# Two heads of a pair on opposite halves of the rows in a chunked RWKV-7 recurrence

## The chip, the cores and the metric

The kernel runs on one core of a Trainium2 chip, in one launch. The metric is the device time of that launch in microseconds (us). PE is the matrix engine with its 128 x 128 array, DVE, ACT and POOL are the vector, scalar and GpSimd engines, and SP issues most of the transfers.

## What is computed

One layer of a hybrid block on x of shape 1 x 2048 x 1024 in float32: an input projection, an S5 branch, an RWKV-7 branch, a gated merge of both, an output projection and a feed-forward layer of width 4096. The change concerns the recurrence of the RWKV-7 branch alone, which has 8 heads of width 64 and goes over 2048 frames:

```python
def step(state, inp):
    rt, wt, kt, vt, at, bt = inp
    sa = jnp.einsum('bhvk,bhk->bhv', state, at)
    state = (state * wt[:, :, None, :] + sa[..., None] * bt[:, :, None, :]
             + vt[..., None] * kt[:, :, None, :])
    yt = jnp.einsum('bhvk,bhk->bhv', state, rt)
    return state, yt
```

Before it stand element-wise steps that make r, the decay, k, v, a and b; behind it a normalization over each head, a bonus term and a gate.

## The kernel before

The program runs in four phases one after the other: `phase_a` (input projection and S5), `phase_b` (the recurrence, and beside it the two gate projections), `phase_c` (merge and output projection) and `phase_d` (feed-forward). Large products are made as three products of split float32 numbers (`mm3`, lines 121 to 123).

`phase_b` goes over 16 steps s of 128 frames, that is two chunks c = 0, 1 of 64 frames. Three generators work on a step, each one step later than the one ahead of it: `elem(s)` makes the operands AR (a and r, scaled by the decay), BK (b and k) and the rest; `inv(s)` makes what depends on one chunk alone; `chain(s)` carries the state. A fourth, `gates()`, makes the products `gp` of the gate projections, 512 columns each and 24 to a bank, from lines 121 to 123. `robin` (line 82) takes one stretch up to the next `yield` from each generator in turn, in the order chain, gates, elem, inv; so the small products of the recurrence stand between gate products on PE. Within a stretch a scheduler may move instructions, except those wrapped in `pin`, which stay in program order and show line 677, the line of the wrapper.

The 8 heads are 4 pairs h with e = 0, 1: head e of a pair has its 64 channels on rows 64e to 64e+63 of AR, BK and the state SB. What `inv(s)` makes for both chunks:

- `m` (line 782): the products of BK with AR of one chunk, 4 pairs by 2 heads, into one bank for each e. The stationary operand is 64 rows (one head's channels) by 128 columns (b and k frames), 128 columns stream. DVE masks them into TM[c] (line 785). The order of b and k in BK turns with c, so chunk 0 has its k frames on rows 0 to 63 and its b frames on rows 64 to 127, chunk 1 the other way round.
- `vt` (line 804): v transposed to frames by channels, all 128 frames and both heads of a pair at once, four products with a 128 x 128 stationary operand and 128 columns. ACT copies 64 rows for each chunk into VU (line 807).
- `NC`, `YC`, `Y`, `X`: the inverse of the chunk's triangular matrix, its 16 x 16 diagonal blocks on DVE (lines 813, 815) by way of transfers through `inv_d`, the rest in `levels(s)` by 64 x 64 and 32 x 32 products P and D.
- `kb` (line 831): the transpose of BK of one chunk to frames by channels, four full 128 x 128 transposes, copied to KB.
- `mv` (line 838): what the chunk's own k and v add, in MV.

`halves(c)` gives the half of the rows that holds the k and v frames of chunk c, and the opposite half, here called its update half, that holds its b frames and the updates u. In the kernel before all 8 heads of a chunk use the same update half. `chain(s)` does for each of the two chunks in turn, n = 2s + c:

- `R` (line 901): four products, one a pair, 128 rows by 64 columns stationary, 128 columns streaming, so that the zeros off the diagonal blocks of SB keep the heads apart. DVE adds MV (line 903) on the 64 rows of the update half, 512 columns.
- `U` (line 907): 8 products of 64 x 64 with Y, all in the one block of the array that has the update half as rows and as columns. ACT copies the 64 rows, 512 columns, into the update half of VU (line 909).
- `S` (line 916), `y` (lines 923, 924): the new state's sum and the outputs, 128 rows by 64 columns stationary, the two heads of a pair in opposite column halves. DVE writes the new state (line 928), POOL has scaled the old one ahead of that (line 898).

The PSUM banks that `m`, `vt`, `kb`, `mv` and some others use come from one pool of two, those of R, U and S from a pool of one.

Of the kernel before, what the change touches and what calls it, by code (L numbers as in the profile page):

```python
# [610 lines left out]
def phase_b(tc, nc, K, io, pm_d, ob_d, h_d, gt_d, gs_d, inv_d):  # L611
    V, A, P, T = nc.vector, nc.scalar, nc.gpsimd, nc.tensor
    NS = S // 128
    with ExitStack() as st:
# [145 lines left out]

        def halves(c):

            return slice(64 * c, 64 * c + 64), slice(64 - 64 * c, 128 - 64 * c)

        def quarters(c):
# [2 lines left out]
        def inv(s):  # L768
# [6 lines left out]
            for c in range(2):  # L775
                tc_ = slice(64 * c, 64 * c + 64)
                mps = [gps(f"m{s}_{c}{e}") for e in range(2)]
                for h in range(4):
                    for e in range(2):
                        er = slice(64 * e, 64 * e + 64)  # L780
                        o = 128 * h
                        pin(T.matmul)(mps[e][:, o:o + 128], BK[er, h, 2 * c:2 * c + 2, :], AR[er, h, :, tc_],
                                      start=True, stop=True)
                for e in range(2):
                    V.tensor_tensor(TM[c][:, :, e], mps[e].rearrange("p (h m t) -> p h m t", h=4, m=2),
                                    msi.unsqueeze(1).to_broadcast([128, 4, 2, 64]), op=ALU.mult)
                yield
            for c in range(2):
# [12 lines left out]
            P.tensor_copy(YC, i16[0:64])  # L801
            vp = gps(f"vt{s}")
            for h in range(4):
                T.matmul(vp[:, 128 * h:128 * h + 128], vm[:, h], cent, start=True, stop=True)
            for c in range(2):
                vc = slice(64 * c, 64 * c + 64)
                A.copy(VU[vc, c, :], vp[vc, :])
# [20 lines left out]
            for c in range(2):  # L828
                kp = gps(f"kb{s}_{c}")
                for h in range(4):  # L830
                    T.transpose(kp[:, 128 * h:128 * h + 128], BK[:, h, 2 * c:2 * c + 2, :].rearrange("p a t -> p (a t)"),
                                K.ident)
                A.copy(KB[:, c, :], kp)
            mv = gps(f"mv{s}")
            for h in range(8):
                for c in range(2):
                    vc, uc = halves(c)
                    pin(T.matmul)(mv[uc, 64 * h:64 * h + 64], TM[c][vc, h // 2, h % 2, 0, :],
                                  VU[vc, c, 64 * h:64 * h + 64], start=True, stop=True)
            MV = ip.tile([128, 512], F32, tag="MV", name=f"MV{s}", bufs=2)  # L840
            A.copy(MV, mv)
# [44 lines left out]
        def chain(s):  # L886
# [2 lines left out]
            yp = psy.tile([128, 512], F32, tag="y", name=f"y{s}")  # L889
            for c in range(2):  # L890
                n = 2 * s + c
                tc_, uc = halves(c)
                S0, S1 = SB[n % 2], SB[(n + 1) % 2]
                if n < 2 * NS - 1:
                    SG = ip.tile([128, 4, 64], F32, tag="SG", name=f"SG{n}", bufs=1)
                    for e in range(2):
                        er = slice(64 * e, 64 * e + 64)
                        P.tensor_tensor(SG[er], S0[er, :, er], gam[er, :, n:n + 1].to_broadcast([64, 4, 64]), op=ALU.mult)
                rp = psc.tile([128, 512], F32, tag="c", name=f"R{n}")
                for h in range(4):  # L900
                    pin(T.matmul)(rp[uc, 128 * h:128 * h + 128], AG[:, c, h, 0], S0[:, h, :], start=True, stop=True)
                R = ip.tile([128, 512], F32, tag="R", name=f"Rs{n}", bufs=2)
                V.tensor_tensor(R[uc, :], rp[uc, :], MV[uc, :], op=ALU.add)
                yield
                up = psc.tile([128, 512], F32, tag="c", name=f"U{n}")
                for h in range(8):
                    T.matmul(up[uc, 64 * h:64 * h + 64], Y[uc, h, :], R[uc, 64 * h:64 * h + 64],
                             start=True, stop=True)
                A.copy(VU[uc, c, :], up[uc, :])
                yield  # L910
                if n < 2 * NS - 1:
                    sp = psc.tile([128, 512], F32, tag="c", name=f"S{n}")
                    for h in range(4):
                        for e in range(2):
                            o = 128 * h + 64 * e
                            T.matmul(sp[64 * e:64 * e + 64, 64 * h:64 * h + 64], KB[:, c, o:o + 64],
                                     VU[:, c, o:o + 64], start=True, stop=True)
                for h in range(4):
                    for e in range(2):
                        er = slice(64 * e, 64 * e + 64)  # L920
                        o = 128 * h + 64 * e
                        yo = yp[er, 128 * h + 64 * c:128 * h + 64 * c + 64]
                        T.matmul(yo, S0[:, h, er], AG[:, c, h, 1], start=True, stop=False)
                        T.matmul(yo, VU[:, c, o:o + 64], TM[c][:, h, e, 1, :], start=False, stop=True)
                if n < 2 * NS - 1:
                    for e in range(2):
                        er = slice(64 * e, 64 * e + 64)
                        V.tensor_tensor(S1[er, :, er], SG[er], sp[er, 0:256].rearrange("p (h t) -> p h t", h=4),
                                        op=ALU.add)
                yield  # L930
# [960 lines left out]
```

## Time and profile before

| | |
|---|---|
| median of 3 runs | 3067.3 us (3063.57 to 3067.74) |
| the profiled execution | 3067.71 us, of which the span from first to last instruction is 3065.8 us |
| mean granted PE clock | 0.975 |
| PE busy | 2915.4 us, 95% of the span |
| DVE, POOL, ACT busy | 62%, 40%, 37% of the span |
| 550 to 1350 us of the span (first to last gate product) | PE busy 736.77 of 800 us |

A row of the profile's groups reads: line, engine, operation, what it writes <- what it reads, shapes, xcount, then busy us and mean ns of one, then the engine's idle time before them and what ended it. In a PE row the first shape, say 64\*128, is the part of the stationary operand that is in use, rows by columns; the second is the streaming operand, rows by columns. A plain float32 product stands as two records, a transpose and a product of split numbers (`gp`) as one; so 8 products of `m` are 16 records. A row of the timeline reads: start us, us to the end of the last, engine, line, operation, xcount; records that overlap are merged, so x16 is 16 records in a row.

### The profile page before, as it was taken

How to read it: one execution, taken by the hardware profiler on the slowest of the kernel's cores; microseconds unless marked ns; L12 is line 12 of the kernel's file. 1: busy time of each engine (PE TensorE's matmuls, PEld its weight loads, DVE VectorE, ACT ScalarE, POOL GpSimd, SP SyncE). 2: the span in 40 equal slices, each digit the busy share in tenths (PEclk: the TensorE clock that was granted, in tenths of full speed). 3: DMA queues.
4: the chain of work that ended last, by engine and by line, in shares of the span. 5: the costliest groups of instructions: out<-in, count | busy, mean ns of one | idle time of the engine just before them, and what ended most of it. 6: DMA issues, size and time to landing. Idle time of an engine off the chain costs nothing.

```text
span 3065.8 us, 45565 instructions
## 1 busy us (share of the span) xinstructions
PE 2915.4 (95%) x17024; PEld 2329.5 (76%) x17024; DVE 1897.8 (62%) x3307; ACT 1121.4 (37%) x1797; POOL 1234.7 (40%) x1082
## 2 busy tenths in 40 slices
PE   8989999689999999999999989999999999999998
PEld 6757777467777777777878778887788788888886
DVE  6366885467777677535322376658655476666667
ACT  5342111234333333234444365555433432222232
POOL 3101101754443343113333345555544565555563
PEclk9999999789999999999999999999999999999999
DMA  4344444755656455367665653333533486666664
GB/s 154 96 132 148 132 148 133 255 187 176 187 167 207 120 149 181 118 195 229 194 213 166 192 188 124 110 110 114 169 113 107 134 240 151 151 151 151 153 146 148
DMA packets 328172, 486.04 MB, mean 159 GB/s; under 512 B 112832, under 2 KB 171712, under 8 KB 327952
## 3 DMA queue, kind: packets, MB, share of 16 engines
q1 hardware_dynamic: 298352, 438.08, 44.8%
q0 software_dynamic: 12960, 40.87, 7.3%
q10 hardware_dynamic: 16640, 4.20, 0.5%
q8 instruction: 134, 2.20, 0.3%
q14 instruction: 86, 0.70, 0.1%
HBM read 327.71 MB, written 147.85 MB: 155 GB/s over the span
## 4 chain that ended last, share of the span: by engine, by line
PE 55%; DVE 10%; DMA 6%; issue 4%; POOL 3%; ACT 2%; SPq 1%; POOLq 0%; DVEq 0%; ACTq 0%
PE s L121 6%; PE s L122 6%; PE s L123 6%; PE f L121 6%; PE f L123 6%; PE f L122 6%; PE gp L121 2%; PE gp L122 2%; PE gp L123 2%; DMA g<-gt_d 1%; PE o L121 1%; DVE yt L813 1%; PE o L122 1%; DVE YC L815 1%; PE o L123 1%
## 5 line engine op out<-in xcount | busy, mean ns | idle before, releaser
L121 PE MATMUL f<-bl,w1h 128*128 128x512 f32 x896 | 354.4, 396 | 9.4 <-ACT w1h L1378 9.3
L122 PE MATMUL f<-bh,w1l 128*128 128x512 f32 x896 | 350.7, 391 | 5.1 <-POOL w1l L1382 5.1
L123 PE MATMUL f<-bh,w1h 128*128 128x512 f32 x896 | 352.1, 393 | 0.0
L121 PE MATMUL s<-w2l,ah 128*128 128x512 f32 x784 | 305.8, 390 | 2.9 <-ACT s L1619 2.9
L122 PE MATMUL s<-w2h,al 128*128 128x512 f32 x784 | 305.7, 390 | 0.0
L123 PE MATMUL s<-w2h,ah 128*128 128x512 f32 x784 | 305.6, 390 | 0.0
L1382 POOL TENSOR_TENSOR w1l<-w1r,w1h 128x512 fp32r<-128x512 f32 x122 | 179.9, 1478 | 180.2 <-ACT w1h L1378 179.8
L121 PE MATMUL gp<-gh,gwh 128*128 128x512 f32 x512 | 225.8, 441 | 21.4 <-ACT gwh L976 14.9
L122 PE MATMUL gp<-gh,gwl 128*128 128x512 f32 x512 | 211.6, 413 | 12.5 <-POOL gwl L977 11.7
L1378 ACT CAST w1h<-w1r 128x512 fp32r<-128x512 f32 x224 | 137.9, 620 | 207.9 <-PE f L123 149.7
L1596 POOL TENSOR_TENSOR al<-ra,ah 128x1024 fp32r<-128x1024 f32 x64 | 168.4, 2634 | 109.2 <-ACT ah L1595 109.0
L123 PE MATMUL gp<-gh,gwh 128*128 128x512 f32 x512 | 209.3, 409 | 0.0
L1626 DVE TENSOR_TENSOR c<-c,s 128x512 f32<-128x512 f32 x224 | 149.9, 684 | 90.5 <-PE s L123 89.8
L121 PEld LDWEIGHTS f<-bl,w1h 128*128 128x128 f32 x896 | 169.4, 189 | 45.7 <-ACT w1h L1378 10.9
L122 PEld LDWEIGHTS f<-bh,w1l 128*128 128x128 f32 x896 | 169.1, 189 | 44.6 <-POOL w1l L1382 7.9
L123 PEld LDWEIGHTS f<-bh,w1h 128*128 128x128 f32 x896 | 168.9, 188 | 38.3
L121 PE MATMUL p<-hl,wh 128*128 128x512 f32 x448 | 183.1, 409 | 0.2
L122 PE MATMUL p<-hh,wl 128*128 128x512 f32 x448 | 178.7, 399 | 0.0
L123 PE MATMUL p<-hh,wh 128*128 128x512 f32 x448 | 178.2, 398 | 0.0
L121 PEld LDWEIGHTS s<-w2l,ah 128*128 128x128 f32 x784 | 147.5, 188 | 33.9 <-ACT s L1619 3.3
L123 PEld LDWEIGHTS s<-w2h,ah 128*128 128x128 f32 x784 | 147.6, 188 | 30.9
L122 PEld LDWEIGHTS s<-w2h,al 128*128 128x128 f32 x784 | 147.5, 188 | 30.6
(392 smaller groups left out, 6778.7 us busy)
## 6 DMA issues: line engine op xcount, KB each, us to landing
w1r<-in_w_dram SPq DMA_DIRECT2D x64, 512.0 KB, 3.5
r_d<-c SPq DMA_DIRECT2D x128, 256.0 KB, 2.0
ra<-r_d SPq DMA_DIRECT2D x64, 512.0 KB, 3.5
gwl<-gs_d SPq DMA_DIRECT2D x48, 512.0 KB, 4.5
gwh<-gs_d SPq DMA_DIRECT2D x48, 512.0 KB, 4.8
ch<-r_d POOLq DMA_DIRECT2D x42, 512.0 KB, 5.7
gt_d<-gs SPq DMA_DIRECT2D x64, 256.0 KB, 5.0
g<-gt_d SPq DMA_DIRECT2D x64, 256.0 KB, 3.4
```

The costliest lines, as they stand in the source:

```text
L121: nc.tensor.matmul(ps, wh, xl, start=start, stop=False)
L122: nc.tensor.matmul(ps, wl, xh, start=False, stop=False)
L123: nc.tensor.matmul(ps, wh, xh, start=False, stop=stop)
L813: V.tensor_tensor(tv, NC[:, 0:k, k:k + 1].to_broadcast([64, k, n]), YC[:, k:k + 1, k:16].to_broadcast([64, k, n]), op=ALU.mult)
L815: V.tensor_tensor(YC[:, 0:k, k:16], YC[:, 0:k, k:16], tv, op=ALU.add)
L1378: cast = A.copy(h, o)
L1382: (P if n % 2 or edge else V).tensor_tensor(l, o, h, op=ALU.subtract)
L1596: P.tensor_tensor(l, raw[n], h, op=ALU.subtract)
L1626: V.tensor_tensor(d, d, bank, op=ALU.add if i in (4, 5, 6) else ALU.subtract)
```

## The change

In a chunk c, head e = 0 of a pair stays where it was, and head e = 1 uses the place that the other chunk's head has: its k, v frames and its updates lie on the opposite half of the rows, as if its chunk were c ^ e. To bring this about:

- `m`: for e = 0 as before; for e = 1 the product of 64 x 128 is cut into two of 64 x 64, b and k apart, that land on swapped halves. The mask writes TM[c ^ e].
- `vt`: the first 64 channels as before, now 64 columns streaming; the second 64 channels in two products with 64 stationary columns each, that land on swapped halves.
- `kb`: for the first 64 channels a transpose of 64 rows by 128 columns with 64 columns streaming; for the second two products of 64 x 64 with the identity, that land on swapped halves.
- `mv`: the same 16 products, their results in other columns, so that a chunk's 8 heads fill 128 rows by 256 columns.
- `R`: 8 products of 64 x 64 with the diagonal blocks of SB alone, in place of four; the two of a pair are in different rows and different columns of the array. The addition of MV has 128 rows by 256 columns.
- `U`: the same 8 products, now pinned, the two of a pair in different rows and different columns. ACT copies in two parts, one for each e.
- `S`, `y`: the same number and shapes, with the indices c ^ e.

Hunks of a blank line and of the header are left out:

```diff
@@ -776,13 +777,14 @@
                 tc_ = slice(64 * c, 64 * c + 64)
                 mps = [gps(f"m{s}_{c}{e}") for e in range(2)]
                 for h in range(4):
-                    for e in range(2):
-                        er = slice(64 * e, 64 * e + 64)
-                        o = 128 * h
-                        pin(T.matmul)(mps[e][:, o:o + 128], BK[er, h, 2 * c:2 * c + 2, :], AR[er, h, :, tc_],
-                                      start=True, stop=True)
+                    o = 128 * h
+                    pin(T.matmul)(mps[0][:, o:o + 128], BK[0:64, h, 2 * c:2 * c + 2, :], AR[0:64, h, :, tc_],
+                                  start=True, stop=True)
+                    for a in range(2):
+                        pin(T.matmul)(mps[1][64 - 64 * a:128 - 64 * a, o:o + 128], BK[64:128, h, 2 * c + a, :],
+                                      AR[64:128, h, :, tc_], start=True, stop=True)
                 for e in range(2):
-                    V.tensor_tensor(TM[c][:, :, e], mps[e].rearrange("p (h m t) -> p h m t", h=4, m=2),
+                    V.tensor_tensor(TM[c ^ e][:, :, e], mps[e].rearrange("p (h m t) -> p h m t", h=4, m=2),
                                     msi.unsqueeze(1).to_broadcast([128, 4, 2, 64]), op=ALU.mult)
                 yield
             for c in range(2):
@@ -801,7 +803,11 @@
             P.tensor_copy(YC, i16[0:64])
             vp = gps(f"vt{s}")
             for h in range(4):
-                T.matmul(vp[:, 128 * h:128 * h + 128], vm[:, h], cent, start=True, stop=True)
+                o = 128 * h
+                T.matmul(vp[:, o:o + 64], vm[:, h], cent[:, 0:64], start=True, stop=True)
+                for c in range(2):
+                    T.matmul(vp[64 * c:64 * c + 64, o + 64:o + 128], vm[:, h, 64 - 64 * c:128 - 64 * c],
+                             cent[:, 64:128], start=True, stop=True)
             for c in range(2):
                 vc = slice(64 * c, 64 * c + 64)
                 A.copy(VU[vc, c, :], vp[vc, :])
@@ -828,14 +834,19 @@
             for c in range(2):
                 kp = gps(f"kb{s}_{c}")
                 for h in range(4):
-                    T.transpose(kp[:, 128 * h:128 * h + 128], BK[:, h, 2 * c:2 * c + 2, :].rearrange("p a t -> p (a t)"),
-                                K.ident)
+                    o = 128 * h
+                    T.transpose(kp[:, o:o + 64], BK[0:64, h, 2 * c:2 * c + 2, :].rearrange("p a t -> p (a t)"),
+                                K.ident[0:64, 0:64])
+                    for a in range(2):
+                        T.matmul(kp[64 - 64 * a:128 - 64 * a, o + 64:o + 128], BK[64:128, h, 2 - 2 * c + a, :],
+                                 K.ident[64:128, 64:128], start=True, stop=True)
                 A.copy(KB[:, c, :], kp)
             mv = gps(f"mv{s}")
             for h in range(8):
                 for c in range(2):
                     vc, uc = halves(c)
-                    pin(T.matmul)(mv[uc, 64 * h:64 * h + 64], TM[c][vc, h // 2, h % 2, 0, :],
+                    o = 256 * (c ^ h % 2) + 64 * (h // 2)
+                    pin(T.matmul)(mv[uc, o:o + 64], TM[c][vc, h // 2, h % 2, 0, :],
                                   VU[vc, c, 64 * h:64 * h + 64], start=True, stop=True)
             MV = ip.tile([128, 512], F32, tag="MV", name=f"MV{s}", bufs=2)
             A.copy(MV, mv)
@@ -889,7 +900,6 @@
             yp = psy.tile([128, 512], F32, tag="y", name=f"y{s}")
             for c in range(2):
                 n = 2 * s + c
-                tc_, uc = halves(c)
                 S0, S1 = SB[n % 2], SB[(n + 1) % 2]
                 if n < 2 * NS - 1:
                     SG = ip.tile([128, 4, 64], F32, tag="SG", name=f"SG{n}", bufs=1)
@@ -898,30 +908,38 @@
                         P.tensor_tensor(SG[er], S0[er, :, er], gam[er, :, n:n + 1].to_broadcast([64, 4, 64]), op=ALU.mult)
                 rp = psc.tile([128, 512], F32, tag="c", name=f"R{n}")
                 for h in range(4):
-                    pin(T.matmul)(rp[uc, 128 * h:128 * h + 128], AG[:, c, h, 0], S0[:, h, :], start=True, stop=True)
-                R = ip.tile([128, 512], F32, tag="R", name=f"Rs{n}", bufs=2)
-                V.tensor_tensor(R[uc, :], rp[uc, :], MV[uc, :], op=ALU.add)
+                    for e in range(2):
+                        er = slice(64 * e, 64 * e + 64)
+                        pin(T.matmul)(rp[halves(c ^ e)[1], 64 * h:64 * h + 64], AG[er, c, h, 0], S0[er, h, er],
+                                      start=True, stop=True)
+                R = ip.tile([128, 256], F32, tag="R", name=f"Rs{n}", bufs=2)
+                V.tensor_tensor(R, rp[:, 0:256], MV[:, 256 * c:256 * c + 256], op=ALU.add)
                 yield
                 up = psc.tile([128, 512], F32, tag="c", name=f"U{n}")
-                for h in range(8):
-                    T.matmul(up[uc, 64 * h:64 * h + 64], Y[uc, h, :], R[uc, 64 * h:64 * h + 64],
-                             start=True, stop=True)
-                A.copy(VU[uc, c, :], up[uc, :])
+                for h in range(4):
+                    for e in range(2):
+                        uc = halves(c ^ e)[1]
+                        pin(T.matmul)(up[uc, 64 * h:64 * h + 64], Y[uc, 2 * h + e, :], R[uc, 64 * h:64 * h + 64],
+                                      start=True, stop=True)
+                for e in range(2):
+                    uc = halves(c ^ e)[1]
+                    A.copy(VU[uc, c ^ e, :].rearrange("p (h e v) -> p h e v", h=4, e=2)[:, :, e, :],
+                           up[uc, 0:256].rearrange("p (h v) -> p h v", h=4))
                 yield
                 if n < 2 * NS - 1:
                     sp = psc.tile([128, 512], F32, tag="c", name=f"S{n}")
                     for h in range(4):
                         for e in range(2):
                             o = 128 * h + 64 * e
-                            T.matmul(sp[64 * e:64 * e + 64, 64 * h:64 * h + 64], KB[:, c, o:o + 64],
-                                     VU[:, c, o:o + 64], start=True, stop=True)
+                            T.matmul(sp[64 * e:64 * e + 64, 64 * h:64 * h + 64], KB[:, c ^ e, o:o + 64],
+                                     VU[:, c ^ e, o:o + 64], start=True, stop=True)
                 for h in range(4):
                     for e in range(2):
                         er = slice(64 * e, 64 * e + 64)
                         o = 128 * h + 64 * e
                         yo = yp[er, 128 * h + 64 * c:128 * h + 64 * c + 64]
                         T.matmul(yo, S0[:, h, er], AG[:, c, h, 1], start=True, stop=False)
-                        T.matmul(yo, VU[:, c, o:o + 64], TM[c][:, h, e, 1, :], start=False, stop=True)
+                        T.matmul(yo, VU[:, c ^ e, o:o + 64], TM[c ^ e][:, h, e, 1, :], start=False, stop=True)
                 if n < 2 * NS - 1:
                     for e in range(2):
                         er = slice(64 * e, 64 * e + 64)
```

The program's order on PE shows what this does to the three groups that are built otherwise. In these rows the last item is what is written, rows by columns; the numbers in the names are those of buffers. First the products `m` of one chunk, in the middle of phase_b; before:

```order
L123 MATMUL gp_8713<-gh_5_6562,gwh_8627 128x512
L677 MATMUL m_00_8789<-AR_8558,BK_8318 128x128
L677 MATMUL m_01_8790<-AR_8558,BK_8318 128x128
...
L907 MATMUL U_8801<-Rs_8763,Y_8376 64x64 x8
L121 MATMUL gp_8713<-gh_6_6564,gwh_8627 128x512
```

and now:

```order
L123 MATMUL gp_9039<-gh_5_6704,gwh_8953 128x512
L677 MATMUL m_00_9119<-AR_8868,BK_8611 128x128
L677 MATMUL m_01_9120<-AR_8868,BK_8611 64x128 x2
L677 MATMUL m_00_9119<-AR_8868,BK_8611 128x128
L677 MATMUL m_01_9120<-AR_8868,BK_8611 64x128 x2
...
L677 MATMUL U_9135<-Rs_9093,Y_8673 64x64 x8
L121 MATMUL gp_9039<-gh_6_6706,gwh_8953 128x512
```

Where 8 products of one shape alternated between the banks m_00 and m_01, a product that writes 128 rows now stands ahead of two that write 64, four times over.

Then the transposes `kb` of both chunks; before:

```order
L937 MATMUL var_9015<-y_8980,cstb 128x512
L831 MATMUL kb_0_9047<-csta,BK_8318 128x128 x4
L123 MATMUL gp_9023<-gh_4_8870,gwh_8709 128x512
...
L121 MATMUL gp_9023<-gh_7_8876,gwh_8709 128x512
L831 MATMUL kb_1_9053<-csta,BK_8318 128x128 x4
L677 MATMUL mv_9059<-VU_8785,TM_8_8787 64x64
```

and now:

```order
L955 MATMUL var_9367<-y_9332,cstb 128x512
L838 MATMUL kb_0_9399<-csta,BK_8611 128x64
L841 MATMUL kb_0_9399<-csta,BK_8611 64x64 x2
L838 MATMUL kb_0_9399<-csta,BK_8611 128x64
L841 MATMUL kb_0_9399<-csta,BK_8611 64x64 x2
...
L121 MATMUL gp_9375<-gh_4_9209,gwh_9035 128x512
...
L838 MATMUL kb_1_9413<-csta,BK_8611 128x64
L841 MATMUL kb_1_9413<-csta,BK_8611 64x64 x2
...
L677 MATMUL mv_9427<-VU_9115,TM_8_9117 64x64
```

The four equal transposes of a chunk have become four times one transpose and two 64 x 64 products, in that alternation, though nothing pins them.

Last the products `vt` with the chain's second R behind them; before:

```order
L924 MATMUL y_8754<-TM_7_8283,VU_8281 64x64
L804 MATMUL vt_8893<-cstb,vm_7769 128x128 x4
L677 MATMUL R_8903<-SB_4598,AG_8153 64x128 x4
L923 MATMUL y_8754<-AG_8153,SB_4598 64x64
L121 MATMUL gp_9023<-gh_0_8862,gwh_8709 128x512
```

and now:

```order
L942 MATMUL y_9080<-TM_7_8572,VU_8569 64x64
L807 MATMUL vt_9232<-cstb,vm_8015 128x64
L809 MATMUL vt_9232<-cstb,vm_8015 64x64 x2
...
L677 MATMUL R_9250<-SB_4598,AG_8437 64x64 x8
L941 MATMUL y_9080<-AG_8437,SB_4598 64x64
L121 MATMUL gp_9375<-gh_0_9201,gwh_9035 128x512
```

Here too one product and two narrower ones alternate, four times, and R has 8 products of 64 x 64 where it had four.

## The prediction

> **What bounds the kernel now.** I read the page first, then the busy time by stretches, then PE's own timeline inside phase_b, then what PE waits for there. The page says that PE is busy nearly throughout:
>
> ```profile
> PE 2915.4 (95%) x17024; PEld 2329.5 (76%) x17024; DVE 1897.8 (62%) x3307; ACT 1121.4 (37%) x1797; POOL 1234.7 (40%) x1082
> ```
>
> The change touches phase_b alone. The stretches (columns: stretch, its length, then PE, PEld, DVE, ACT and POOL busy, PE clock, DMA share, GB/s) put its steady part at
>
> ```profile
> 585.00:1335.00 750.00, 702.67 (x7256) 545.64 (x7255) 519.75 (x1034) 246.38 (x422) 283.80 (x359) 0.97 0.55 167
> ```
>
> So PE bounds this phase too: 702.67 of 750 us, against 519.75 on DVE, and 47.3 us is all the idle time there is. [...] The list of waits says what the 47.3 us are; these are the nine lines in which PE waits for a transfer or for a long chain on DVE or POOL (the columns are the total, the times, the longest):
>
> ```profile
> PE P L677 <- DVE X L825: 12.9, 6, 5.1
> PE m L677 <- DVE bv L757: 6.9, 4, 3.7
> PE gp L121 <- DMA gh<-h_d: 4.6, 5, 1.6
> ...
> PE gp L122 <- POOL gwl L977: 2.5, 2, 2.1
> PE bo L753 <- DVE ys L952: 2.0, 1, 2.0
> PE gp L121 <- DMA gwh<-gs_d: 1.8, 2, 1.2
> ...
> PE bo L753 <- DVE sq L738: 1.4, 2, 1.1
> ...
> PE m L677 <- DVE yt L813: 0.9, 1, 0.9
> ...
> PE m L677 <- DVE ys L952: 0.2, 1, 0.2
> ```
>
> They sum to 33.2 us. The other 14 us are short waits for a step that PE itself has just fed.
>
> **What a change of shape costs.** A stretch of PE's timeline in which nothing waits:
>
> ```profile
> 955.20 0.39 PE L123 MATMUL gp<-gh,gwh 128*128 128x512 f32 x1
> 955.52 1.16 PE L677 MATMUL m<-AR,BK 64*128 64x128 f32 x16
> 956.61 1.14 PE L907 MATMUL U<-Rs,Y 64*64 64x64 f32 x16
> 957.68 0.50 PE L121 MATMUL gp<-gh,gwh 128*128 128x512 f32 x1
> 958.01 0.39 PE L122 MATMUL gp<-gh,gwl 128*128 128x512 f32 x1
> 958.24 0.40 PE L123 MATMUL gp<-gh,gwh 128*128 128x512 f32 x1
> ```
>
> Gate products in a row start 0.23 us apart (958.01 to 958.24). From gp to m it is 0.32, so 0.09 more. A record of U alone lasts 0.22 (its group's mean, quoted below), so the last of the 16 starts at 956.61 + 1.14 - 0.22 = 957.53, and they are (957.53 - 956.61)/15 = 0.061 apart; from there to gp it is 0.15, again 0.09 more, and the next gp comes 0.33 after it, 0.10 late. Leaving one stationary shape for another costs 0.09, and the second record behind the change is late too: by 0.10 if 128 columns have to be loaded. For 64 columns it is half of that, by the next rows: R's 8 records take 963.04 to 963.97 = 0.93, which is 8 x 0.11 + 0.05.
>
> ```profile
> 961.95 1.16 PE L804 MATMUL vt<-cstb,vm 128*128 128x128 f32 x8
> 963.04 1.09 PE L677 MATMUL R<-SB,AG 128*64 128x128 f32 x8
> 963.97 0.28 PE L923 MATMUL y<-AG,SB 128*64 128x64 f32 x2
> ```
>
> R and y have one shape, 128\*64, and between them nothing is lost. [...]
>
> The trace even shows one product of `m` cut off between other shapes, as the change will do to all of them:
>
> ```profile
> 690.11 0.24 PE L881 MATMUL D<-Y,Ps 32*32 32x32 f32 x2
> 690.28 0.48 PE L677 MATMUL m<-AR,BK 64*128 64x128 f32 x2
> 690.69 0.28 PE L881 MATMUL D<-Y,Ps 32*32 32x32 f32 x6
> ```
>
> From its start to the start of what follows: 0.41 us. In the run of 8 above it was (956.61 - 955.52)/8 = 0.14.
>
> What alternating between halves is worth is there as well:
>
> ```profile
> 960.36 0.34 PE L916 MATMUL S<-VU,KB 128*64 128x64 f32 x4
> ...
> 974.23 0.60 PE L831 MATMUL kb<-csta,BK 128*128 128x128 f32 x4
> 974.76 1.15 PE L677 MATMUL mv<-VU,TM 64*64 64x64 f32 x32
> 975.84 0.38 PE L946 MATMUL gt<-sgx,g 128*128 128x128 f32 x1
> ```
>
> `mv`, whose 64 x 64 products alternate between two blocks of the array with no row and no column in common, does 32 records in the time in which U, in one block, does 16.
>
> **The change part by part.** A pair of narrow products in opposite halves, cut off between other shapes: the first four records of S start within 0.34 - 0.22 = 0.12, and leaving costs 0.15 (U to gp), so 0.27 for 64 streaming columns. For 128, both passes are 0.05 longer (R's 0.11 against U's 0.06): 0.37.
>
> - `m`: each of the 4 pairs is now one 64\*128 product cut off (0.41) and a cut-off pair of 64\*64 (0.37). 4 x 0.78 = 3.12 where 1.09 stood. 32 groups: 32 x 2.03 = **+65**.
> - `vt`: the first product has 64 streaming columns, so 0.41 - 0.10 = 0.31; the pair 0.27. 4 x 0.58 = 2.32 where 963.04 - 961.95 = 1.09 stood. 16 x 1.23 = **+20**.
> - `kb`: the transpose is one record, so no second one is late: 0.15 to the next start; the pair 0.27. 4 x 0.42 = 1.68. Ahead of `mv` 974.76 - 974.23 = 0.53 stood, and `mv` now follows in the same shape, which gives back 0.14; but entering from gp now costs 0.09: +1.1. Between gate products the group began in their own shape and cost 0.44 (four times 0.11); now 1.68 and 0.19 for coming and going: +1.43. 16 of each: **+41**.
> - `R`: 16 records in alternating blocks, as half of `mv` with the leaving, 0.62, where 0.93 stood; where a gate product follows the saving is 0.10 more, where y follows it pays for a change of shape, 0.14. I take -0.36 on average between -0.17 and -0.41: 32 x -0.36 = **-11**.
> - `U`: 0.62 for 957.68 - 956.61 = 1.07: 32 x -0.45 = **-14**.
> - `mv`, `S`, `y`: the same products, the same shapes: 0.
>
> ```profile
> L907 PE MATMUL U<-Rs,Y 64*64 64x64 f32 x512 | 36.5, 221 | 2.5 <-DVE Rs L903 2.5
> ...
> L903 DVE TENSOR_TENSOR Rs<-R,MV 64x512 f32<-64x512 f32 x32 | 22.0, 688 | 49.6 <-PE R L677 49.2
> ...
> L928 DVE TENSOR_TENSOR SB<-SG,S 64x256 f32<-64x256 f32 x62 | 25.8, 416 | 33.8 <-PE S L916 32.8
> L909 ACT COPY VU<-U 64x512 f32<-64x512 f32 x32 | 18.6, 582 | 69.5 <-PE U L907 69.4
> ...
> L875 ACT COPY Ps<-P 32x256 f32<-32x256 f32 x32 | 11.7, 365 | 58.7 <-PE P L871 58.3
> ```
>
> - The addition after R has 256 columns in place of 512: 416 ns instead of 688, 0.27 less on the chain, 32 times. PE's own waits for it are 2.5 us in all, and that bounds what it can give; I take 0 to -2.5, and -1 goes into the rounding.
> - The copy after U is two of 256 columns, 2 x 365 = 730 ns for 582. What covers the 0.15 is the gate products that stand between U and S; without that cover it costs 32 x 0.15 = 5. I take 0.
>
> PE's own work: 65 + 20 + 41 - 11 - 14 = **+101 us**, nearly all of it from some 560 new changes of shape inside groups (7 in each of 32 + 16 + 32).
>
> What of this lies beside a wait? PE becomes 13% slower in this phase while transfers, DVE and POOL have the same work, so the waits for them should close: -33.2, the nine lines. The 14 us of short waits stay, since what feeds them is PE. Net 101 - 33 = +68. No later phase is touched; they begin later. The profiled execution took 3067.71 us, 1.9 more than its span and 0.4 more than the median, so the sum is 3067.7 + 68 = **3136 us**.
>
> Ends: with all 47.3 of idle time closed it is 3121; if half of the lateness of second records hides as well (0.10 for each of 192 wide products of `m` and `vt`, 0.05 for each of 320 pairs, 35 in all), 3104. With nothing closed it is 3169.
>
> **Rivals.**
>
> *The chain sets the pace (faster).* Where a step's chain R, add, U, copy is what PE waits for, the change takes 0.36 + 0.27 + 0.45 - 0.15 = 0.93 off each of 32 chunks: 30 us, so 3038. The place is the wait of U and S in `chain`. It decides only if a change of shape costs next to nothing: without it the streams alone would be +15 (`m`, a third product of 0.12 for each of 128 pairs), +8 (`kb`), -25, about even; at over 30/560 = 0.05 us a change the gain is gone. The rows show 0.09 and more, in both directions and between five shapes, and PE's waits for this chain are 2.5 us. 4%.
>
> *The cut-off pairs do not overlap.* The two 64\*64 products of `m`, and of `kb`, read the same rows of the array and differ in columns alone, and no row shows that for 64 rows. If the second waits for the first, each pair costs two more records: 0.22 x 128 for `m`, 0.11 x 192 for `vt` and `kb`, +49, so 3185. Against it: S does just this with 128 rows, four records within 0.12. [...] 12%.
>
> *The waits close further.* PE's idle time falls to nothing and the clock, 0.97 in this phase, comes up with it: 3121 or a little under. For it: PE gets slower by twice the idle time. Against it: the short waits are for steps that PE feeds. 12%.
>
> *Nothing measurable.* All the new work falls into idle time: there is 47 us of it for 101 us. 1%.
>
> The forecast itself has 71%.
>
> **How the numbers follow.** The likeliest value is 3136. The range goes from the lower end, 3104, to a little over the case of pairs without overlap, 3188; the faster rival and that of nothing measurable lie outside it. A measurement of this kernel can tell about 0.2%, 6 us, from no change. Faster: the first rival, 4%. Same: the fourth and a sliver of the third, 2%. Slower: 94%.
>
> **What would show it.** In the new profile the groups `m`, `vt` and `kb` should take about 3.1, 2.3 and 1.7 us from first start to the next group's, R and U about 0.6 each; PE's idle time in phase_b should fall from 47 to about 14 us, and the last gate product should start near 1417 instead of 1349 us. If `m` takes under 2 us the price of a change of shape is wrong; if it takes 4, the pairs do not overlap. If these lengths are right and the time is not, the closing of the waits was misjudged.

## The result and the profile after

The changed kernel takes 3188.83 us (median of 4 runs, 3181.93 to 3198.63) against 3067.52 (4 runs, 3063.57 to 3069.61): a ratio of 1.0399, 95% interval 1.037 to 1.0429, or 121 us slower. The forecast was 3136. The profiled execution is the slowest of the four: 3198.63 us, span 3196.6, mean granted clock 0.953; the other three had 0.959 or 0.960. One of the later runs of the kernel before, at 4076.0 us with a granted clock of 0.652, is a slow one and stands in no median below.

The page says that PE is still busy nearly throughout, with 152 us more than before:

```profile
PE 3067.3 (96%) x18304; PEld 2418.1 (76%) x18304; DVE 1888.1 (59%) x3307; ACT 1127.3 (35%) x1829; POOL 1230.5 (38%) x1082
```

The last gate product starts at 1486.45 instead of 1349.00, 137.5 later, and what follows is 6.6 us shorter; so all of the loss is in phase_b. The steady part of that phase, now 870 us long (columns as in the prediction):

```profile
585.00:1455.00 870.00, 840.91 (x8269) 623.40 (x8270) 501.41 (x1023) 246.89 (x441) 283.67 (x358) 0.88 0.46 141
```

Two things differ from the forecast. The clock is 0.88 where 0.97 stood, and idle time is 870 - 840.91 = 29.1 us, not 14. What PE waits for most, from 585 to 1460:

```profile
PE P L677 <- DVE X L831: 9.7, 5, 5.4
PE m L677 <- DVE bv L757: 6.6, 4, 4.4
PE m L677 <- DVE TM L787: 2.7, 3, 1.3
```

The wait for `X`, 12.9 before, and that for `bv`, 6.9, have hardly closed.

The products themselves are as long as forecast. PE's timeline at two groups `m`:

```profile
760.01 0.68 PE L677 MATMUL R<-SB,AG 64*64 64x64 f32 x16
760.63 0.50 PE L122 MATMUL gp<-gh,gwl 128*128 128x512 f32 x1
...
761.29 3.08 PE L677 MATMUL m<-AR,BK 64*128 64x128 f32 x22
...
765.70 0.63 PE L122 MATMUL gp<-gh,gwl 128*128 128x512 f32 x1
766.13 0.63 PE L123 MATMUL gp<-gh,gwh 128*128 128x512 f32 x1
...
767.97 3.19 PE L677 MATMUL m<-AR,BK 64*128 64x128 f32 x24
771.09 0.93 PE L934 MATMUL S<-VU,KB 128*64 128x64 f32 x16
```

The first of these two groups ends mixed with the products U, left out here. The second takes 771.09 - 767.97 = 3.12 us, the forecast to the digit, and R 0.62. But between the two groups the gate products start 0.43 apart instead of 0.23. The stretches over the same place, 3.4 us each, show why (the clock is the third number from the right):

```profile
761.10:764.50 3.40, 3.40 (x35) 2.21 (x35) 1.20 (x2) 0.68 (x2) 3.39 (x2) 1.00 0.82 289
764.50:768.00 3.50, 3.50 (x21) 2.34 (x18) 1.97 (x4) 2.65 (x4) 3.50 (x7) 0.51 0.38 153
768.00:771.40 3.40, 3.40 (x35) 2.23 (x36) 0.56 (x1) 1.25 (x3) 1.64 (x3) 0.99 0.00 0
771.40:774.80 3.40, 3.40 (x47) 3.09 (x43) 3.32 (x7) 0.00 (x0) 1.73 (x2) 0.50 0.13 14
774.80:791.80 17.00, 17.00 (x167) 12.73 (x165) 7.71 (x34) 6.66 (x11) 1.77 (x4) 1.00 0.69 224
```

A stretch that `m` fills (761.10, 768.00) has a clock of 1.00 or 0.99, and the one behind it of 0.51 or 0.50. PE has no idle time in any of them. The stretches are cut, to a tenth, at the changes of the clock that this trace records: 764.54, 767.95, 771.36 and 774.78. The traces of the kernel before and of this one hold 46 and 80 records of the clock; in each of them it is 1.0 or 0.5, and all changes of one trace lie a whole number of times 3.4133 us apart, to within 0.005 us. A stretch between two lines of this measured grid is called a window below. The transposes do the same:

```profile
729.05 0.39 PE L123 MATMUL gp<-gh,gwh 128*128 128x512 f32 x1
729.37 0.27 PE L838 MATMUL kb<-csta,BK 64*128 64x64 f32 x1
729.58 0.33 PE L841 MATMUL kb<-csta,BK 64*64 64x64 f32 x4
729.84 0.27 PE L838 MATMUL kb<-csta,BK 64*128 64x64 f32 x1
...
732.95 1.28 PE L677 MATMUL mv<-VU,TM 64*64 64x64 f32 x31
```

```profile
730.40:733.80 3.40, 3.40 (x60) 2.66 (x61) 3.24 (x8) 1.17 (x2) 0.55 (x1) 1.00 0.33 108
733.80:737.20 3.40, 3.40 (x20) 3.09 (x16) 2.82 (x6) 0.58 (x1) 1.73 (x3) 0.50 0.40 102
```

Here the groups of both chunks stand back to back, 732.95 - 729.37 = 3.58 us of alternation, and half clock follows. The last of the three groups built otherwise, `vt`:

```profile
1048.23 0.43 PE L807 MATMUL vt<-cstb,vm 128*128 128x64 f32 x2
1048.60 0.34 PE L809 MATMUL vt<-cstb,vm 128*64 128x64 f32 x4
1048.86 0.43 PE L807 MATMUL vt<-cstb,vm 128*128 128x64 f32 x2
```

A pair of heads takes 0.63 here where 0.58 was forecast, because a wide product with 64 columns takes 0.37 instead of 0.31.

In the kernel before, half clock follows idle time too: PE is busy for 1.10 of the 3.42 us up to 1005.62, and from there to 1015.86 the clock is 0.50. There 32 records of P take 1.97 us behind 5.07 us of idle time; at a clock of 1.00 they take 1.15 (`e4_kb_cut` at 772.82):

```profile
1009.58 1.97 PE L677 MATMUL P<-X,TM 64*64 64x64 f32 x32 [5.07 <-DVE X L825]
```

But it isn't the cause in the rows above: in the windows ahead of that half clock (761.10, 768.00 and 730.40) PE is busy for 3.40 of 3.40 us.

### The profile page after: what moved, and what is told of

It reads as the page before. It is cut to its first block, busy times and chain, and to the rows that moved or that the text cites. A ratio compares the mean times of both kernels' runs of the same rounds, so it can differ in the third digit from the quotient of the medians.

```text
span 3196.6 us, 48189 instructions
## 1 busy us (share of the span) xinstructions
PE 3067.3 (96%) x18304; PEld 2418.1 (76%) x18304; DVE 1888.1 (59%) x3307; ACT 1127.3 (35%) x1829; POOL 1230.5 (38%) x1082
## 4 chain that ended last, share of the span: by engine, by line
PE 62%; DVE 7%; DMA 6%; issue 2%; POOL 2%; ACT 2%; SPq 0%; POOLq 0%; DVEq 0%; ACTq 0%
PE f L121 6%; PE f L123 6%; PE f L122 6%; PE s L122 5%; PE s L123 5%; PE s L121 5%; PE m L677 3%; PE gp L121 3%; PE gp L122 3%; PE gp L123 3%; DMA g<-gt_d 2%; DMA wor<-in_wout_dram 2%; PE kb L841 1%; DVE bl L1369 1%; PE vt L807 1%
## 5 line engine op out<-in xcount | busy, mean ns | idle before, releaser
L121 PE MATMUL gp<-gh,gwh 128*128 128x512 f32 x512 | 235.3, 460 | 17.0 <-ACT gwh L994 17.0
L122 PE MATMUL gp<-gh,gwl 128*128 128x512 f32 x512 | 220.0, 430 | 13.8 <-POOL gwl L995 11.6
L123 PE MATMUL gp<-gh,gwh 128*128 128x512 f32 x512 | 216.4, 423 | 0.0
```

What stands on the lines that cost most here:

```text
L121: nc.tensor.matmul(ps, wh, xl, start=start, stop=False)
L122: nc.tensor.matmul(ps, wl, xh, start=False, stop=False)
L123: nc.tensor.matmul(ps, wh, xh, start=False, stop=stop)
```

## The experiments

The theories, with the letters used in the expectations. **A**: behind some 3 us in which nearly all is changes of shape, PE is granted half the clock, and that is what the forecast lacks. **B**: narrow products lower the clock by themselves, since they use a quarter of the array. **C**: the added time is neither, but waits on banks or copies. **F**: the clock goes with the number of changes, wherever they stand. **D**, formed later: the waits stay open because the first transfers of `inv` leave later. **E**, its rival: the pool of banks and the second copy of `kb`, or the order of products as such, keep them open. All kernels compute the whole layer. Beside the first four the kernel before took 3065.05 us (median of 7), beside the next four (`e5` to `e8`) 3062.14 (22 runs), beside the last four 3064.46 (7).

### The new layout in one shape

`e1_one_shape` is the changed kernel with `m` and `kb` in 64 x 64 products alone and `vt` in 128 x 64 alone; `kb` goes into two banks, with two copies.

```diff
-                    pin(T.matmul)(mps[0][:, o:o + 128], BK[0:64, h, 2 * c:2 * c + 2, :], AR[0:64, h, :, tc_], ...)
                     for a in range(2):
+                        pin(T.matmul)(mps[0][64 * a:64 * a + 64, o:o + 128], BK[0:64, h, 2 * c + a, :], ...)
                         pin(T.matmul)(mps[1][64 - 64 * a:128 - 64 * a, o:o + 128], BK[64:128, h, 2 * c + a, :], ...)
```

> The changed kernel with m, vt and kb each built in one stationary shape (m as sixteen 64x64 products on four blocks of the array, vt as sixteen of 128x64, kb as sixteen of 64x64 into two banks), the layout on opposite halves kept. Theory A (a change of shape costs 0.15 to 0.2 us, and where a stretch of 3 to 4 us consists of such changes the granted clock falls to half): no changes inside groups, so PE has about 19 us less work than before the change (R and U -25, kb +6), the clock is back at 0.97 or more, and the time is 3045 us (3030 to 3065). Theory B (the clock falls because so many products use a quarter of the array, in whatever order): the clock stays at 0.96 or below and the time is 3090 us or more. Theory C (the added time is waits on banks or copies): two banks for kb and two copies make it no better than 3130 us.

Measured: 3092.04 us, ratio 1.0083 (1.0054 to 1.0112). It has more and narrower products than the changed kernel, and yet the mean clock of its runs is 0.970 to 0.976, where the kernel before has 0.975 to 0.978 and the changed one 0.953 to 0.960. From 700 to 1300 us, before, after and `e1`:

```profile
700.00:1300.00 600.00, 569.22 (x6040) 441.69 (x6037) 430.32 (x886) 202.82 (x350) 221.56 (x293) 0.98 0.54 165
```

```profile
700.00:1300.00 600.00, 578.94 (x5816) 429.66 (x5813) 359.21 (x726) 177.28 (x315) 205.87 (x273) 0.88 0.48 145
```

```profile
700.00:1300.00 600.00, 534.08 (x7359) 405.51 (x7360) 410.86 (x828) 198.15 (x380) 210.74 (x278) 0.96 0.53 158
```

Here `m` takes 0.93 us:

```profile
971.48 1.10 PE L677 MATMUL m<-AR,BK 64*64 64x128 f32 x32
972.41 0.82 PE L677 MATMUL U<-Rs,Y 64*64 64x64 f32 x16
```

The time, 3092, is what B expected, but the clock tells against B. Half clock begins 13 times in `e1` between 585 and 1455 us, and 10 times in the kernel before, each time behind a window with idle time in it (0.19 of the window or more). In the changed kernel it begins 28 times, and 21 of these follow a window with less than a tenth idle. So B falls, and C, no better than 3130, with it. But A had expected a time below before, 3045, and 534.08 of 600 busy shows that PE now idles more: its wait for `X` is up from 12.9 us.

```profile
PE P L677 <- DVE X L832: 33.6, 11, 5.5
```

### The same products, sorted by shape

`e2_wide_first` has all products of the changed kernel, but in `m`, `vt` and `kb` the four wide ones first and the narrow ones behind them, all pinned in that order (cut to `m`):

```diff
                 for h in range(4):
                     o = 128 * h
                     pin(T.matmul)(mps[0][:, o:o + 128], ...)
+                for h in range(4):
+                    o = 128 * h
                     for a in range(2):
```

> The changed kernel with the same products in another order: in each group of m, vt and kb all wide products first, then all narrow ones, so one change of shape inside a group where there were seven. Theory A: a group of m 2.15 us, of vt 1.35, of kb 1.0; over the kernel before that is +34, +4 and +18, less 25 for R and U, less some 15 of waits: 3085 us (3070 to 3110), clock 0.97. Theory B: the same number of narrow products, so the clock stays at 0.96 and the time is 3130 us. Theory C: no change from 3189 us beyond 20 us.

Measured: 3095.21, ratio 1.0098 (1.0068 to 1.0127), clock 0.95 from 700 to 1300; `m` takes 2.11 (up to the S behind it), `vt` 1.55, `kb` 0.88 us.

```profile
748.40 2.18 PE L677 MATMUL m<-AR,BK 64*128 64x128 f32 x24
```

That is 30 us above the kernel before where the changed kernel is 121 above it: the order alone, with no product added or taken, is worth 91 us.

### One cut at a time, in the kernel before

`e3_m_cut` cuts the second head's `m` into two of 64 x 64 (to the same rows as before), `e4_kb_cut` does the same to `kb`, `e6_vt_cut` to `vt`; all else is the kernel before. For `e3`:

```diff
-                    for e in range(2):
-                        er = slice(64 * e, 64 * e + 64)
-                        pin(T.matmul)(mps[e][:, o:o + 128], BK[er, h, 2 * c:2 * c + 2, :], AR[er, h, :, tc_], ...)
+                    pin(T.matmul)(mps[0][:, o:o + 128], BK[0:64, h, 2 * c:2 * c + 2, :], AR[0:64, h, :, tc_], ...)
+                    for a in range(2):
+                        pin(T.matmul)(mps[1][64 * a:64 * a + 64, o:o + 128], BK[64:128, h, 2 * c + a, :], ...)
```

> The kernel before with one part of the change alone: m's products of the second head cut in two 64x64 products, landing where they landed before, so wide and narrow alternate in m. Theory A: +65 us of PE work, less some 25 of waits, and the clock falls in the 3.1 us groups of m, to about 0.965, which costs another 30: 3135 us (3110 to 3155). Theory B: half as many narrow products are added as in the whole change and the drop is less than half: clock 0.97, 3110 us. Theory C: under 3090 us.

> The kernel before with another part alone: kb's transposes cut as in the change (a transpose of 64x128 and two products of 64x64, alternating), landing where they landed before. Theory A: +47 us of PE work (0.46 us for each pair of heads), less some 20 of waits; the groups are 1.9 us long, shorter than those of m, so the clock falls less, to 0.970: 3105 us (3085 to 3125). Theory B: clock 0.965 or below, since kb adds as many narrow products as m. Theory C: under 3085 us.

> The kernel before with vt alone cut as in the change (a product of 128x128 and two of 128x64, alternating), landing where they landed before. 2.41 us a group instead of about 1.0: +22 us of PE work in 16 groups, less some 7 of waits. Theory A (the clock falls where 3 to 4 us are mostly changes of shape): groups of 2.4 us, but only 16 of them, so the clock falls little, to 0.973: 3085 us (3072 to 3098). If the parts add up, m (+76), kb (+45), vt (+20) and R and U with the rest (-20) give the whole change's +121 to +124.

Measured: `e3` 3141.44 (1.0233, 1.0194 to 1.0272), `e4` 3109.86 (1.0142, 1.0109 to 1.0174), `e6` 3081.51 (1.0065, 1.0045 to 1.0085). The three stretches, in that order:

```profile
700.00:1300.00 600.00, 578.81 (x5395) 435.62 (x5392) 386.30 (x783) 183.38 (x311) 212.20 (x279) 0.90 0.50 152
```

```profile
700.00:1300.00 600.00, 573.53 (x5919) 445.36 (x5915) 408.74 (x824) 191.54 (x324) 216.96 (x281) 0.94 0.51 155
```

```profile
700.00:1300.00 600.00, 573.33 (x6135) 445.27 (x6134) 417.76 (x852) 197.66 (x340) 219.76 (x285) 0.98 0.53 162
```

The groups of `m` (3.12 us) and the double groups of `kb` (3.57 us or more, back to back in 14 of 16 steps) go with a lower clock, 0.90 and 0.94 where the kernel before has 0.98, the group of `vt` (2.4 us, 0.98) does not. Alone the three cost 76, 45 and 19 us, in sum 140. The whole change costs 121. If the parts simply add, which was not tried, what is left of it is worth about -20: R and U (forecast: -25), and whatever the layout adds in waits.

### Breaking the run of changes

`e9_kb_cut_apart` is `e4` with one turn of the gate products between the two groups of `kb`; `e10_kb_apart` is the kernel before with that turn alone. `e11_m_cut_gap` and `e12_m_gap` are the like for `m`, with the turn in the middle of the group.

```diff
                 A.copy(KB[:, c, :], kp)
+                if c == 0:
+                    next(gg, None)
```

> The kernel with kb alone cut (3110 us; its clock in 700 to 1300 us of the span 0.94, where the kernel before has 0.98). There the groups of both chunks stand back to back, 3.5 us of alternation in 14 of 16 steps. Here one stretch of six gate products is drawn from the gates' generator between the two, so that every group is 1.7 us long and fenced by gate products; the same products, about 5% more changes of shape. Theory A (the clock falls where 3 to 4 us in a row are mostly changes of shape): the clock in 700 to 1300 us is back at 0.97 or more, and the time in that part falls accordingly; the whole may not, since the gates' products run out some 22 us earlier and leave the end uncovered: 3100 us (3085 to 3115). Theory F (the clock loss goes by the number of changes, wherever they stand): 0.94 as before.

> The control for it: the kernel before, uncut, with the same stretch of gate products between kb's two groups. Both theories: clock 0.98 in 700 to 1300 us; the time shows what drawing gate products earlier costs by itself, 3065 us (3060 to 3080).

> The kernel with m alone cut (3141 us, clock 0.90 in 700 to 1300 us), with six gate products drawn between the second and the third pair of heads of each group of m, without a yield, so that the other generators keep their places. Most groups of 3.1 us become two runs of 1.5 us with 1.4 us of gate products between; the number of changes is the same within 2%. Theory A: clock 0.95 or more in 700 to 1300 us. Theory F: 0.90. The gate products run out some 45 us earlier, so the end of the phase will be uncovered and the whole time says little: 3120 to 3170 us.

> The control for it: the kernel before, m uncut, with the same six gate products between its second and third pair of heads. Both theories: clock 0.97 or more in 700 to 1300 us; the time shows the cost of drawing the gate products earlier, 3085 us (3070 to 3110).

Measured: `e9` 3090.65 (1.01, 1.0072 to 1.0127) beside its control `e10` 3080.61 (1.0051, 1.0036 to 1.0067): 10 us for the cut, where `e4` paid 45. `e11` 3176.26 (1.0368, 1.034 to 1.0397) beside `e12` 3124.31 (1.0196, 1.0181 to 1.0212): 52 us, where `e3` paid 76. `e9` has every change of shape that `e4` has:

```profile
894.42 0.27 PE L832 MATMUL kb<-csta,BK 64*128 64x64 f32 x1
...
896.28 0.50 PE L121 MATMUL gp<-gh,gwh 128*128 128x512 f32 x1
...
897.88 0.27 PE L832 MATMUL kb<-csta,BK 64*128 64x64 f32 x1
```

and yet, `e9` and then `e11`:

```profile
700.00:1300.00 600.00, 581.56 (x6218) 448.89 (x6218) 417.21 (x833) 195.44 (x334) 214.01 (x283) 0.99 0.54 164
```

```profile
700.00:1300.00 600.00, 582.28 (x5611) 437.37 (x5608) 370.29 (x750) 185.80 (x319) 213.09 (x284) 0.95 0.53 162
```

Runs of 1.86 us with six gate products between them leave the clock at 0.99 (`e4` 0.94, `e10` 0.97), and `m` in halves of 1.5 us brings it from 0.90 to 0.95 (`e12` 0.97). F falls. The 35 and 24 us are not the clock's alone, since the turn also shifts gate products: it costs 16 us by itself in `e10` and 60 in `e12`, where they run out early (the last one starts at 1341.1, while the chain's last outputs come at 1391). Both costs are above what was expected of the controls, 3065 (3060 to 3080) and 3085 (3070 to 3110), and `e11` lies above its range too.

A stands, but the length of a run is not the whole of it: what goes with half clock in these traces is how much of one window it fills. Two double groups of `kb` in `e4`, cut at the grid of its trace; the first runs from 714.83 to 718.50, the second from 760.41 to 764.12:

```profile
714.80:718.20 3.40, 3.40 (x37) 2.43 (x36) 3.26 (x7) 0.59 (x1) 0.39 (x1) 1.00 0.27 69
718.20:721.60 3.40, 3.40 (x42) 3.17 (x43) 3.33 (x6) 1.17 (x2) 1.27 (x1) 0.50 0.43 121
759.10:762.60 3.50, 3.50 (x32) 2.37 (x30) 3.16 (x12) 1.50 (x3) 0.00 (x0) 1.00 0.48 176
762.60:766.00 3.40, 3.40 (x55) 2.62 (x54) 3.37 (x3) 1.21 (x3) 1.65 (x2) 1.00 0.79 192
766.00:769.40 3.40, 3.40 (x21) 2.92 (x20) 2.28 (x5) 0.33 (x1) 0.42 (x1) 1.00 0.57 154
```

The first fills 0.98 of a window, and half clock follows. The second is as long, but a line of the grid divides it, into 0.63 and 0.46 of two windows, and the clock stays whole. Of the 28 double groups of `e4` and the changed kernel, the 14 that fill 0.74 or more of one window are followed by half clock, the 14 that fill 0.72 or less are not. In `e9` no window is filled beyond 0.54, and a group of `vt`, 2.41 us, can fill 0.71 at most. For `m` the limit is less sharp: in `e3` and the changed kernel half clock follows every window that it fills to 0.8 or more, and some below (counted to the start of what follows, in the changed kernel those filled to 0.78 at 1194.62 and to 0.52 at 873.76, but not that of 0.79 at 1307.26).

`e7_m_cut_split` was the first try at this: `e3` with a `yield` in the middle of the group.

```diff
+                    if h == 1:
+                        yield
```

> The kernel with m alone cut (3141 us, clock 0.962) with a yield after the second pair of heads, so that most groups of m fall into two runs of half the length with gate products or other work between them; the products and, within 1%, the number of changes of shape stay the same. Theory A (what counts for the clock is how much of a stretch of 3 to 4 us the array spends in changes): the clock comes back to about 0.970 and the time to 3118 us (3105 to 3130). Theory F (the clock loss goes by the number of changes, wherever they stand): clock 0.962, 3140 us.

Measured: 3218.24 (1.051, 1.0488 to 1.0532), slower than `e3`. The extra `yield` makes rounds of `robin` longer, so gate products run out at 1433 while the chain goes on to 1483, and PE waits longer for `X` (3.7 us in `e3`):

```profile
PE P L677 <- DVE X L828: 34.0, 3, 17.2
```

Its mean clock, 0.949 to 0.953, is below what either theory expected. But between 585 and 1455 us half clock begins 13 times, and each time behind a window with 0.22 or more of idle time, so this run can't tell A from F.

### Why the waits stay open

In the new layout each TM[c] takes one head of a pair from each chunk, so the transfers of chunk 0 need the masks of both. The timelines, before, then the changed kernel, then `e1` (in square brackets: idle time ahead of the row, and what ended it):

```profile
914.97 1.29 DVE L785 TENSOR_TENSOR TM<-m,cstb 128x512 f32<-128x512 f32 x2 [0.96 <-PE m L677]
916.29 5.47 SPq L791 DMA_DIRECT2D inv_d<-TM  x8
918.72 1.29 DVE L785 TENSOR_TENSOR TM<-m,cstb 128x512 f32<-128x512 f32 x2 [2.46 <-PE m L677]
```

```profile
764.95 1.28 DVE L787 TENSOR_TENSOR TM<-m,cstb 128x512 f32<-128x512 f32 x2
770.84 1.29 DVE L787 TENSOR_TENSOR TM<-m,cstb 128x512 f32<-128x512 f32 x2 [4.26 <-PE m L677]
771.55 4.45 SPq L793 DMA_DIRECT2D inv_d<-TM  x8
```

```profile
831.62 1.28 DVE L787 TENSOR_TENSOR TM<-m,cstb 128x512 f32<-128x512 f32 x2
834.54 1.29 DVE L787 TENSOR_TENSOR TM<-m,cstb 128x512 f32<-128x512 f32 x2 [1.64 <-PE m L677]
835.26 4.11 SPq L793 DMA_DIRECT2D inv_d<-TM  x8
```

The transfers start 1.3 us after the first mask before, 6.6 after it in the changed kernel, 3.6 in `e1` (medians of the 16 steps: 1.4, 7.4 and 4.7). `e5_by_slot` is `e1` with `m` grouped by the TM that it feeds, so that the first group makes all of TM[0]; `e8_by_slot_one_bank` is `e5` with `kb` as sixteen 128 x 64 products in one bank, with one copy, by the estimate in its expectation 14 us more work on PE.

```diff
-                        pin(T.matmul)(mps[0][64 * a:64 * a + 64, o:o + 128], BK[0:64, h, 2 * c + a, :], ...)
-                        pin(T.matmul)(mps[1][64 - 64 * a:128 - 64 * a, o:o + 128], BK[64:128, h, 2 * c + a, :], ...)
+                        for e in range(2):
+                            er = slice(64 * e, 64 * e + 64)
+                            b = c ^ e
+                            r0 = 64 * (a ^ e)
+                            pin(T.matmul)(mps[e][r0:r0 + 64, o:o + 128], BK[er, h, 2 * b + a, :], ...)
-                V.tensor_tensor(TM[c ^ e][:, :, e], ...)
+                V.tensor_tensor(TM[c][:, :, e], ...)
```

> The one-shape kernel of the first experiment (3092 us) with the products of m grouped by the slot they fill and not by the chunk: the first group makes head 0 of chunk 0 and head 1 of chunk 1, all that TM[0] holds, the second the rest. In the layout of the change each TM needs the masks of both chunks, so the transfers of the first half leave only after the second mask (5.2 us after the first mask starts, against 1.4 before), and PE waits longer for X. Theory D (that delay is what ate the gain of the one-shape kernel): the first transfer leaves at about 1.5 us again, PE's wait for X falls from 34 to about 20 us, time 3070 us (3055 to 3080). Theory E (the bank pool and the two copies of kb ate it, or the order of products as such): no better than 3085 us.

> The same with kb in one bank and one copy: sixteen products of 128x64 with half of the identity, 1.05 us a chunk where two banks take 0.6. PE work 32 x 0.45 = 14 us more than with two banks. Theory D: 3080 us, slower than with two banks, less what the waits take up. Theory E with the bank pool as the cause: faster than with two banks, under 3070 us.

Measured: `e5` 3065.68 (1.0012, 0.9999 to 1.0026, 12 runs), `e8` 3063.13 (1.0003, 0.9991 to 1.0016, 11 runs). The first transfer of `e5` starts 1.3 us after the first mask again (the median), the wait for `X` is shorter by 10 us (33.6 in `e1`), and the time is 3.5 us above the kernel before where that of `e1` was 27.0 above it:

```profile
PE P L677 <- DVE X L833: 23.2, 12, 5.1
```

So D holds for these kernels; that it keeps the changed kernel's own wait open is likely, since its first transfer leaves even later, but was not tried by itself. `e8` came out as E expected, under 3070, and not near 3080 as D did: by that estimate it has more work on PE than `e5`, and it is no slower. Either that work falls where PE would wait, or the one bank and the one copy pay for it; these runs can't tell which. Neither kernel beats the one before.

## Why the prediction was right and wrong

- **The price of a change of shape** held: 0.09 and the late second record gave `m` 3.12 (3.12 forecast), R and U 0.62, `kb` 1.72 to 1.86 (1.68, without coming and going) and `vt` 2.41 (2.32). Only a wide product with 64 streaming columns was under-sized, by 0.06. The sum of +101 for PE's own work was short by some 3: 16 x 0.09 for `vt`, and 16 x (3.57 - 3.50) for the two groups of `kb` with their coming and going.
- **The pairs overlap.** The second rival is false: the four records of a pair in the same rows start within 0.33 - 0.22 = 0.11 (729.58, `kb`, above), where four records in one block, 0.061 apart as in U, would take 0.18. That this rival's figure, 3185, is so close to the 3188.83 measured is chance.
- **The clock is the step that failed.** The prediction named the clock, 0.97, only as something that might come up, and priced everything at it. It went down to 0.88. From the profiled execution: 137.5 us later at the last gate product, less 104 of work, plus 18 of waits that closed, leaves some 52; this is a remainder, and no run measures it by itself. The bound from above is 0.09 x 870 = 78. So the mechanism foreseen, changes of shape, was right, and what came with it here, half clock behind a window that they fill (0.51 and 0.50 at 764.50 and 771.40), was missed. The sorted order shows how much hangs on it together with the changes: 91 of 121 us.
- **The closing of the waits** was over-sized: idle time went from 47.3 to 29.1, which is 18 and not 33 (from the first to the last gate product 62.5 to 44.6, also 18). The step said that transfers, DVE and POOL have the same work; they have, but the first transfer now needs a mask of the second chunk, which is the likely reason. By the list of waits the long ones, 33.2 before, still make 22.8, and the short ones, which the step had kept at 14, shrank to 6.5. The third rival, that all waits close, falls with it. The two misses, 52 and 15, with the 3 above, are more than the 53 between 3136 and 3188.83, because the profiled execution is 9.8 above the median and what follows phase_b is shorter by 6.6.
- **The chain** (first rival) does not set the pace as far as these runs show: `e5` and `e8` have the shorter chain and hardly a change of shape inside groups, and are only level with the kernel before.
- What the prediction said would show it: the lengths right and the time wrong was to mean that the closing of the waits was misjudged. That is about a fifth of it (15 of 70); the clock was not on the list.

What stays open: what it is in a run of changes that the clock answers to, since no row of these profiles shows it; and windows where `m` mixes with other small products, some of which are followed by half clock at 0.5 to 0.6 (in the changed kernel 0.52 at 873.76, 0.56 at 976.16). Alternation between two full-width shapes was not tried.

## What to carry to other kernels

Sort products by the shape of their stationary operand before counting them: here the same products cost 91 us more in alternation. Where alternation can't be avoided, try breaking it up with products like those of the gates: double groups of `kb` that filled 0.74 or more of a window of 3.413 us were followed by a clock of 0.50, and cut apart, with 0.54 at most (`e9`), they left it at 0.99 from 700 to 1300 us. Read the granted clock of the new order in short stretches rather than taking over that of the old. A layout that shortens a chain may tie two chunks together, as here, where the first transfer left 7.4 us after the first mask instead of 1.4: look at when the first transfer of each can leave.

## What the hardware showed that was not expected

- Half clock with PE busy throughout: in the changed kernel stretches of 3.4 us at 0.50 or 0.51 behind a stretch that alternation filled, and in `e9` 0.99 from 700 to 1300 us with runs of 1.86 us. In `e4` a run of 3.71 us, divided into 0.63 and 0.46 of two windows, was followed by 1.00.
- Products on four blocks of 64 x 64: 32 records of 128 columns in 0.93 us (`e1`), against 16 records in 1.09 as 64 x 128 in the kernel before.
